# Attention of a transformer block on one core: pairs of heads in five pieces, projections in pieces of 24 products, one written order on TensorE, modulation vectors behind the projections

## The chip, the cores and the metric

The kernel runs on one core of a Trainium2 chip. A core has TensorE (PE in the profile), VectorE (DVE), ScalarE (ACT), GpSimd (POOL) and SyncE (SP), which here does nothing but issue loads. Each engine works through its own queue in order. The metric is the time of one execution on the device in microseconds (us); lower is better.

## The reference, cut to what matters

The program is a block of two layers over 256 latent and 256 context tokens with a model width of 1024. The first layer mixes by attention, the second by a gated recurrence (hgrn); each has a gated feed-forward part behind it (ffn). Modulation vectors, six for each layer, come from a condition vector:

```python
def ada_mod(cvec, w, b):
    return jnp.split(jax.nn.silu(cvec) @ w + b, 6, axis=-1)

q, k, v = jnp.split(h @ w_qkv, 3, axis=-1)         # 16 heads of 64
q = rms_norm(q.reshape(B, n, NA_HEADS, NA_HEAD_DIM), q_gain) * scale
k = rms_norm(k.reshape(B, n, NA_HEADS, NA_HEAD_DIM), k_gain)
...
s = jnp.einsum('bqhd,bkhd->bhqk', q_c, k_c)         # context tokens
p = jax.nn.softmax(s.astype(jnp.float32), axis=-1).astype(v_c.dtype)
o_c = jnp.einsum('bhqk,bkhd->bqhd', p, v_c)
out_ctx = o_c.reshape(B, h_ctx.shape[1], D_MODEL) @ w_o
...
s = jnp.concatenate([s_loc.reshape(B, NA_HEADS, GRID_W, n_loc), s_ctx], axis=-1)   # latent tokens
p = jax.nn.softmax(s.astype(jnp.float32), axis=-1).astype(v_win.dtype)
return (jnp.einsum('bhqjw,bjqwhd->bqhd', p_loc, v_win)
        + jnp.einsum('bhqk,bkhd->bqhd', p[..., n_loc:], v_c))
```

A latent token looks at a window of latent tokens, with a bias from a table, and at all context tokens; a context token looks at the context alone. Everything is in 32-bit floats.

## The kernel before

A 32-bit product is made of three matmuls on numbers split into a high and a low part (`prod`, high by high, high by low, low by high). "A product" below is one such matmul. The weights come by DMA as `w_raw` (1 MB for 1024 rows by 256 columns), are cast by ScalarE to `w_hi` and subtracted by DVE to `w_lo` (`weights`, `split`).

`na` is the attention. The 16 heads are handled as 8 pairs, in four groups g of two pairs. A group needs 256 columns each of q, k and v: for each of these, `toks` makes four token tiles of 24 products (8 tiles of the depth by 3), two token tiles to a bank of PSUM. The q and k banks are then normalized: ScalarE squares (`qk_sq`), DVE sums (`qk_ss`), takes an inverse root in nine small steps (`rsqrt`) and multiplies. v is copied by ScalarE. Group 0's columns are made earlier, in `setup`, and stand in banks (`early`).

`na_pair` does two heads. PE transposes q and k (8 transposes), ScalarE and DVE write the split `qs`, `ks`, `ql`. Then for each head a `chain`: scores of two query tiles against all 512 keys (`logits`, 8 matmuls of 512 columns for the pair), addition of the bias and minimum by DVE, exponential by ScalarE, scaling by DVE; 16 transposes of the probabilities (`turned`, copied to `pt_l` by ScalarE or DVE); scores of the context queries (8 matmuls of 256 columns), softmax, 8 transposes and a copy to `pt_c`; last the probabilities on the values (L651, L659) into a bank `o`, of which `oh` and `ol` are the high and low parts.

`ada` makes one modulation vector m of a layer. SP loads 8 tiles of 512 KB (`ada_raw`) into the pool `apool`, which has two buffers. For each tile PE makes four matmuls of 256 columns (L216; the trace lists 8 passes for a tile), side by side on four column groups. At the end DVE copies the row, PE transposes it (L228), and `ada_put` adds the bias. Before, `NA_ADA=((2,), (4,), (), (3,))` says which vector is made after which group: vector 2 with group 0, 4 with group 1, none with group 2, 3 with group 3.

Behind the groups stands the out-projection: its products (512 columns) multiply `w_o` and `oh`, `ol` of all eight pairs. Its product for pair k needs only that pair.

The order on the engines is not the order of the code. A scheduler of the framework takes the instructions by program order as a priority and by its own estimate of when operands are ready, and lets later products slip between the steps of attention. In the order that results before, products of the next group's projections and modulation steps stand singly and in small groups between the matmuls of attention, and the rest of a group's projections stand in a row ahead of the next group.

## Time and profile before

| | before |
|---|---|
| median of three runs | 1173.29 us |
| runs | 1167.57, 1173.29, 1173.75 us |
| profiled execution, time | 1168.13 us |
| profiled execution, span from first to last instruction | 1166.3 us |
| TensorE busy | 1138.9 us, 98% of the span |
| VectorE busy | 778.7 us, 67% |
| ScalarE busy | 501.7 us, 43% |
| 16 DMA engines | 145 GB/s on the mean |

"Busy" is the time in which an engine worked on at least one instruction. Matmuls overlap each other, so the mean length of one in the profile is more than the distance from one to the next; where density matters, the distance from start to start in the timeline is to be read. An execution takes some 2 us more than its span. All rows below are from the profiled execution, and times in them count from the start of its span.

### The profile page before, as it was taken

The page shows a single profiled execution, that of the slowest core. Times are in us where ns is not written, and L with a number is a line of the kernel's source. Part 1 is how long each engine was busy: PE and PEld are TensorE (multiplying, and loading weights), DVE is VectorE, ACT ScalarE, POOL GpSimd, SP SyncE. Part 2 cuts the span into 40 slices and gives each one's busy share as a digit, 9 for nine tenths or more (in the row PEclk, how much of TensorE's full clock was granted, in tenths as well). Part 3 has the DMA queues.
Part 4 walks back from the last instruction along what each step waited for, and adds up shares of the span by engine and source line. Part 5 has one row for each costly group of instructions (what it writes and reads, how often), then busy time and mean ns, then how long its engine had stood idle before and what let it go on. Part 6 is the DMA issues. An engine that isn't in the chain of part 4 may idle for free.

```text
span 1166.3 us, 21342 instructions
## 1 busy us (share of the span) xinstructions
PE 1138.9 (98%) x8539; PEld 987.2 (85%) x8539; DVE 778.7 (67%) x1872; ACT 501.7 (43%) x1079; POOL 74.5 (6%) x121
## 2 busy tenths in 40 slices
PE   6979989999999999999999999999999999999998
PEld 5968869887898787878887889889797988999998
DVE  4579776966697664845353778686768687556553
ACT  5356564745462232213223344434243465545442
POOL 1045331410000000000000000000000000000000
PEclk9999999999999999999999999999999999999999
DMA  9785452433337442636352651323232345564562
GB/s 330 252 211 94 118 131 73 64 130 124 107 93 229 135 170 94 230 136 216 130 194 68 199 167 46 100 74 110 73 110 74 99 175 197 182 210 158 197 217 87
DMA packets 134403, 169.23 MB, mean 145 GB/s; under 512 B 4609, under 2 KB 122273, under 8 KB 134305
## 3 DMA queue, kind: packets, MB, share of 16 engines
q1 hardware_dynamic: 132368, 164.64, 42.5%
q0 software_dynamic: 1728, 3.17, 3.2%
q8 instruction: 67, 1.10, 0.4%
q14 instruction: 32, 0.25, 0.1%
q10 hardware_dynamic: 208, 0.07, 0.0%
HBM read 166.82 MB, written 1.05 MB: 144 GB/s over the span
## 4 chain that ended last, share of the span: by engine, by line
PE 90%; DVE 4%; DMA 3%; ACT 2%; issue 1%; ACTq 0%; DVEq 0%
PE mm L410 49%; PE ax L410 28%; DMA ada_raw<-in_ada_w_dram 3%; PE ada_ps L216 2%; PE ax L651 2%; PE ax L902 1%; PE ax L613 1%; PE ax L579 1%; PE ax L637 1%; PE ax L885 1%; PE ax L580 1%; PE ada_ps L266 1%; ACT qs L569 1%; DVE w_lo L403 1%; PE ax L948 1%; PE ax L659 1%
## 5 line engine op out<-in xcount | busy, mean ns | idle before, releaser
L403 DVE TENSOR_TENSOR w_lo<-w_raw,w_hi 128x512 fp32r<-128x512 f32 (+1 forms) x448 | 272.5, 644 | 128.4 <-ACT w_hi L402 126.0
L402 ACT CAST w_hi<-w_raw 128x512 fp32r<-128x512 f32 (+1 forms) x448 | 238.0, 583 | 230.6 <-PE mm L410 100.3
L410 PE MATMUL mm<-hl,w_hi 128*128 128x256 f32 (+1 forms) x608 | 201.6, 333 | 0.0
L410 PE MATMUL mm<-hh,w_lo 128*128 128x256 f32 (+1 forms) x608 | 201.3, 332 | 0.0
L410 PE MATMUL mm<-hh,w_hi 128*128 128x256 f32 (+1 forms) x608 | 199.1, 329 | 0.0
L410 PE MATMUL ax<-hh,w_lo 128*128 128x256 f32 (+1 forms) x400 | 131.7, 330 | 0.0
L410 PE MATMUL ax<-hh,w_hi 128*128 128x256 f32 (+1 forms) x400 | 131.7, 329 | 0.0
L410 PE MATMUL ax<-hl,w_hi 128*128 128x256 f32 (+1 forms) x400 | 131.3, 328 | 0.0
L410 PE MATMUL mm<-w_hi,hh 128*128 128x256 f32 x448 | 126.3, 282 | 0.8 <-ACT hh L366 0.8
L410 PE MATMUL mm<-w_lo,hh 128*128 128x256 f32 x448 | 125.7, 280 | 0.0
L410 PE MATMUL mm<-w_hi,hl 128*128 128x256 f32 x448 | 125.5, 280 | 0.0
L410 PEld LDWEIGHTS mm<-hl,w_hi 128*128 128x128 f32 x608 | 114.1, 188 | 11.4
L410 PEld LDWEIGHTS mm<-hh,w_lo 128*128 128x128 f32 x608 | 114.0, 188 | 11.3
L410 PEld LDWEIGHTS mm<-hh,w_hi 128*128 128x128 f32 x608 | 113.8, 188 | 10.9 <-ACT hh L366 0.8
L319 DVE SCALAR_TENSOR_TENSOR ada_acc<-ada_raw,cs,ada_acc 128x1024 f32<-128x1024 f32 x63 | 79.0, 1280 | 19.4 <-DMA ada_raw<-in_ada_w_dram 19.2
L410 PEld LDWEIGHTS mm<-w_hi,hh 128*128 128x128 f32 x448 | 84.6, 189 | 5.1 <-issue 3.2
L410 PEld LDWEIGHTS mm<-w_hi,hl 128*128 128x128 f32 x448 | 84.2, 188 | 2.0 <-issue 1.6
L410 PEld LDWEIGHTS mm<-w_lo,hh 128*128 128x128 f32 x448 | 84.2, 188 | 1.8 <-issue 1.4
L410 PEld LDWEIGHTS ax<-hh,w_hi 128*128 128x128 f32 x400 | 75.2, 188 | 7.6 <-ACT w_hi L402 0.8
L410 PEld LDWEIGHTS ax<-hl,w_hi 128*128 128x128 f32 x400 | 75.1, 188 | 7.4
L410 PEld LDWEIGHTS ax<-hh,w_lo 128*128 128x128 f32 x400 | 74.9, 187 | 7.4 <-DVE w_lo L403 0.2
L696 ACT CAST mid_h<-sa 128x512 fp32r<-128x512 f32 (+1 forms) x44 | 22.5, 512 | 92.8 <-DVE sa L693 92.8
(278 smaller groups left out, 2133.3 us busy)
## 6 DMA issues: line engine op xcount, KB each, us to landing
w_raw<-in_ffn_w_in_dram SPq DMA_DIRECT2D x44, 1024.0 KB, 5.1
ada_raw<-in_ada_w_dram SPq DMA_DIRECT2D x80, 512.0 KB, 4.6
w_raw<-in_hg_w_in_dram SPq DMA_DIRECT2D x20, 1024.0 KB, 4.8
w_raw<-in_na_w_qkv_dram SPq DMA_DIRECT2D x9, 1024.0 KB, 5.0
ada_first<-in_ada_w_dram SPq DMA_DIRECT2D x32, 256.0 KB, 5.9
w_raw<-in_ffn_w_out_dram SPq DMA_DIRECT2D x8, 896.0 KB, 4.5
w_raw<-in_ffn_w_out_dram SPq DMA_DIRECT2D x8, 768.0 KB, 4.3
w_raw<-in_ffn_w_out_dram SPq DMA_DIRECT2D x8, 640.0 KB, 4.3
```

The source lines that it names most:

```text
L216: nc.tensor.matmul(ps[32 * j : 32 * j + 32, 0:256], cs[:, k, :], w[:, j * 256 : (j + 1) * 256], start=(k == 0), stop=(k == last), tile_pos ...
L266: nc.tensor.matmul(ps[32 * j : 32 * j + 32, 0:P], self.cs[:, k, :], w[:, j // 2, (j % 2) * P : (j % 2 + 1) * P], start=(k == 0), stop=(k = ...
L319: eng.scalar_tensor_tensor(acc[s], w, c, acc[s], op0=ALU.mult, op1=ALU.add)
L402: self.nc.scalar.copy(wh[:, ks], raw[:, ks])
L403: self.nc.vector.tensor_tensor(wl[:, ks], raw[:, ks], wh.bitcast(F32)[:, ks], op=ALU.subtract)
L410: self.nc.tensor.matmul(out, a, b, start=(start and i == 0 and j == 0), stop=(stop and i == n - 1 and j == 2), skip_group_check=True,)
L569: nc.scalar.activation(cap(qa[half], P - 1, back), src, AF.Copy, scale=self.q_gain[own])
L579: nc.tensor.matmul(ps, qs[a][:, t], ks[a][:, kr], start=True, stop=False, skip_group_check=True)
L580: nc.tensor.matmul(ps, self.ql[a][:, t], ks[a][:, kr], start=False, stop=True, skip_group_check=True)
L613: nc.tensor.transpose(tp[:, kt * P : (kt + 1) * P], sb[:, kt * P : (kt + 1) * P], self.ident)
L651: nc.tensor.matmul(o[64 * a : 64 * a + 64, 0:256], v[:, kt, j * P + 64 * a : j * P + 64 * a + 64], pts[a][0][:, kt], start=(kt == 0), stop ...
L696: nc.scalar.copy(mh, sa)
```

## The change

`na_pair` becomes a generator that gives way four times and so has five pieces: (1) the transposes of q and k with what ScalarE and DVE make of them; (2) the local scores and softmax of both heads; (3) the 16 transposes of the probabilities, the context scores and their softmax; (4) the context transposes; (5) the probabilities on the values. Within a piece both heads follow each other.

`pieces` cuts the projections of groups 1 to 3 into 36 pieces of 24 products, in the order v, q, k for each group, and gives `ada_steps(0, (2, 4, 3))` behind them. That makes the three modulation vectors of attention in twelve steps of two tiles (8 matmuls); its first turn only loads the first two tiles, and each step asks for the next two tiles behind its own matmuls. The pool has two buffers as before.

`na` then writes out which pieces of projections stand between which pieces of pairs: four before the first scores, and in a group 2, 2, 1, 1, 2, 1, 1 and 2 (`fill`). So groups 0 and 1 hold 12 pieces of projections each, group 2 has 8 and then the first modulation steps, and group 3 has the rest of these. The first piece of the next group's first pair stands in the second half of the group, between piece 3 and piece 4 of its second pair.

`in_order` adds to every PE instruction of this part an order dependency on the one before it. So PE's order is the written one there. The early projections and the out-projection are not in that list; the out-projection's products are still placed by the scheduler.

```diff
-NA_ADA = ((2,), (4,), (), (3,))
...
+    def ada_steps(self, l, params):
...
+        def pair(m, k):
+            ws = []
+            for e in range(2):
+                w = self.apool.tile([P, D], F32, name="ada_raw", tag="ada_raw")
+                nc.sync.dma_start(w, self.in_ada_w[l, (k + e) * P : (k + e + 1) * P, m * D : (m + 1) * D])
+                ws.append(w)
+            return ws
+
+        todo = [(m, k) for m in params for k in range(0, KT, 2)]
+        ws, turn = pair(*todo[0]), None
+        yield
+        for n, (m, k) in enumerate(todo):
+            if k == 0:
+                ps = self.psum.tile([P, T], F32, tag="ada", name="ada_ps", bufs=1)
+            for e, w in enumerate(ws):
+                for j in range(4):
+                    nc.tensor.matmul(
...
+            if n < len(todo) - 1:
+                ws = pair(*todo[n + 1])
+            if k == KT - 2:
+                row = self.spool.tile([P, 256], F32, name="ada_row", tag="ada_row", bufs=1)
+                nc.vector.tensor_copy(row, ps[:, 0:256])
+                yield
+                for b in range(2):
+                    nc.tensor.transpose(ps[:, 256 + b * P : 256 + (b + 1) * P], row[:, b * P : (b + 1) * P], self.ident)
+                self.ada_put(l, m, 0, 4, ps[:, 256:512], 0)
+            else:
+                yield
...
+    def in_order(self, first):
+
+        ins = [i for i in self.nc.cur_bb.bb.instructions[first:] if i.engine == mybir.EngineType.PE]
+        for i, j in zip(ins[:-1], ins[1:]):
+            self.tc.add_manual_dep(
+                j, i.name, mybir.DependencyInfo(mybir.DependencyClass.NoSync, mybir.DependencyReason.DATA),
+                reason="in_order",
+            )
...
+        blocks = [(g, i) for g in range(1, 4) for i in (2, 0, 1)]
...
+        def pieces():
+            load(0)
+            for n, (g, i) in enumerate(blocks):
+                for tt in range(4):
+                    if tt % 2 == 0:
+                        banks[g, i, tt // 2] = self.mm()
+                    self.toks(banks[g, i, tt // 2][:, tt % 2 * 256 : tt % 2 * 256 + 256], loaded[n], tt)
+                    if tt == 0:
+                        load(n + 1)
+                    yield
+            yield from self.ada_steps(0, (2, 4, 3))
...
+        for i in range(2):
+            for b in range(2):
+                normed(0, i, b)
+        for b in range(2):
+            values(0, b)
+        fill(2)
+        pair = [self.na_pair(np_, pr, done, oh, ol) for pr in range(2 * 4)]
+        next(pair[0])
+        values(1, 0)
+        fill(2)
+        values(1, 1)
         for g in range(4):
...
+            one, two = pair[2 * g : 2 * g + 2]
+            next(one)
+            fill(2)
+            next(one)
+            fill(2)
+            next(two)
+            next(one)
+            if g < 3:
                 for b in range(2):
...
+                    normed(g + 1, 0, b)
+            fill(1)
+            next(one, None)
+            fill(1)
+            if g < 3:
+                normed(g + 1, 1, 0)
+            next(two)
+            fill(2)
+            if g < 3:
+                normed(g + 1, 1, 1)
+            next(two)
+            fill(1)
+            if g < 3:
+                next(pair[2 * g + 2])
+            next(two)
+            fill(1)
+            next(two, None)
+            if g < 2:
+                values(g + 2, 0)
+            fill(2)
+            if g < 2:
+                values(g + 2, 1)
+        assert next(steps, steps) is steps
+        self.in_order(first)
```

What the change does to the order is seen best in three places. In these listings the line numbers are those of the kernel that is listed; L410, L554, L216, L637 and L651 of before are L445, L661, L322, L746 and L759 of the changed kernel, and `x4` means four in a row.

The first place is PE in the middle of attention, where the second pair of a group ends and the first pair of the next group begins (`ident,qk` are transposes of q and k, `ident,sbc` context transposes, `pt_l,v` probabilities on values). Before:

```order
L637 MATMUL ax_2702<-ident,sbc 128x128 x2
L651 MATMUL ax_2718<-pt_l,v 64x256 x4
L659 MATMUL ax_2718<-pt_c,v 64x256 x4
L554 MATMUL ax_2752<-ident,qk_2168 128x128 x4
L554 MATMUL ax_2753<-ident,qk_2315 128x128 x4
L410 MATMUL mm<-w_lo,hh_158 128x256
```

And the changed kernel:

```order
L445 MATMUL mm<-w_lo,hh_164 128x256
L445 MATMUL mm<-w_hi,hl_172 128x256
L661 MATMUL ax_2495<-ident,qk_2140 128x128 x4
L661 MATMUL ax_2496<-ident,qk_2253 128x128 x4
L746 MATMUL ax_2519<-ident,sbc 128x128 x4
L746 MATMUL ax_2525<-ident,sbc 128x128 x4
L445 MATMUL mm<-w_hi,hh_157 128x256
```

The transposes of the next group's q and k, which stood behind the last products on values of a group, now stand ahead of the context transposes, right behind a piece of products.

The second place is PE in the last group, whose modulation steps are `ada_raw,cs`; `oh` and `ol` are products of the out-projection. Before, near the transposes of the last pair:

```order
L554 MATMUL ax_3329<-ident,qk_2915 128x128 x4
L554 MATMUL ax_3330<-ident,qk_3062 128x128 x4
L216 MATMUL ada_ps<-ada_raw,cs 32x256 x8
L410 MATMUL mm<-oh_863,w_hi 128x512
L410 MATMUL mm<-ol_871,w_hi 128x512
```

And the changed kernel there, from the end of the seventh pair's context scores on:

```order
L688 MATMUL ax_3399<-ks_3215,ql_880 128x256
L322 MATMUL ada_ps<-ada_raw,cs 32x256 x16
L661 MATMUL ax_3458<-ident,qk_2887 128x128 x4
L661 MATMUL ax_3459<-ident,qk_2988 128x128 x4
L746 MATMUL ax_3482<-ident,sbc 128x128 x4
L746 MATMUL ax_3488<-ident,sbc 128x128 x4
L322 MATMUL ada_ps<-ada_raw,cs 32x256 x8
L759 MATMUL ax_3508<-pt_l,v 64x256 x8
L759 MATMUL ax_3508<-pt_c,v 64x256 x4
L333 MATMUL ada_ps<-ident,ada_row 128x128 x2
L322 MATMUL ada_ps<-ada_raw,cs 32x256 x8
```

Four steps (one step is x8) now stand in the stretch that had one.

The third place is the queue of SP from the start of attention on (`L298` and `L310` are loads of modulation tiles for attention). Before:

```order
L395 DMA w_raw<-in_na_w_qkv_dram 128x8x256 x2
L298 DMA ada_raw<-in_ada_w_dram 128x1024 x4
L395 DMA w_raw<-in_na_w_qkv_dram 128x8x256
L298 DMA ada_raw<-in_ada_w_dram 128x1024 x4
L395 DMA w_raw<-in_na_w_qkv_dram 128x8x256 x2
L395 DMA w_raw<-in_na_w_o_dram 128x8x256 x3
```

And the changed kernel:

```order
L430 DMA w_raw<-in_na_w_qkv_dram 128x8x256 x7
L430 DMA w_raw<-in_na_w_o_dram 128x8x256 x3
L310 DMA ada_raw<-in_ada_w_dram 128x1024 x2
L430 DMA w_raw<-in_na_w_o_dram 128x8x256
L310 DMA ada_raw<-in_ada_w_dram 128x1024 x20
```

The loads of modulation tiles, which stood among those of weights, now stand in a row behind them.

## Rows read from the trace of the kernel before

**Rows 1.** The page's busy times: us, share of the span, instructions.
```profile
PE 1138.9 (98%) x8539; PEld 987.2 (85%) x8539; DVE 778.7 (67%) x1872; ACT 501.7 (43%) x1079; POOL 74.5 (6%) x121
```

**Rows 2.** The page's chain that ended last, by engine and line.
```profile
PE mm L410 49%; PE ax L410 28%; DMA ada_raw<-in_ada_w_dram 3%; PE ada_ps L216 2%; PE ax L651 2%; PE ax L902 1%; PE ax L613 1%; PE ax L579 1%; PE ax L637 1%; PE ax L885 1%; PE ax L580 1%; PE ada_ps L266 1%; ACT qs L569 1%; DVE w_lo L403 1%; PE ax L948 1%; PE ax L659 1%
```

**Rows 3.** Stretches of attention: length, busy us (instructions) of each engine, clock, DMA.
```profile
195.50:250.90 55.40, 54.95 (x434) 48.71 (x433) 43.93 (x130) 33.48 (x72) 16.57 (x20) 1.00 0.35 72
250.90:291.00 40.10, 40.04 (x271) 27.68 (x269) 27.42 (x71) 25.67 (x58) 0.00 (x0) 1.00 0.40 132
sum 229.00, PE 218.98 PEld 177.78 DVE 174.81 ACT 128.36 POOL 67.82; mean PE 43.80 PEld 35.56 DVE 34.96 ACT 25.67 POOL 13.56
```

**Rows 4.** Waits from 62 to 291 us: total us, times, longest.
```profile
PE ada_ps L216 <- DMA ada_raw<-in_ada_w_dram: 9.1, 6, 2.6
```

**Rows 5.** Waits of SP's own queue in the same stretch.
```profile
SPq L298 <- PE ada_ps L216: 39.0, 14, 10.7
SPq L298 <- DMA ada_raw<-in_ada_w_dram: 28.9, 10, 8.4
```

**Rows 6.** PE's timeline (start, us, operation): first transposes of groups 2 and 3.
```profile
195.47 1.03 PE L554 MATMUL ax<-ident,qk 128*128 128x128 f32 x8
...
249.22 0.28 PE L410 MATMUL mm<-w_hi,hh 128*128 128x256 f32 x1
...
250.93 1.03 PE L554 MATMUL ax<-ident,qk 128*128 128x128 f32 x8
```

**Rows 7.** Group 2's operations on PE by form: count, busy us, mean ns.
```profile
L410 PE MATMUL mm<-w_lo,hh 128*128 128x256 f32 x97 | 27.1, 280 | 0.0
```

**Rows 8.** PE's timeline around a modulation step of the last group.
```profile
264.78 0.28 PE L579 MATMUL ax<-ks,qs 128*128 128x256 f32 x1
264.90 0.28 PE L580 MATMUL ax<-ks,ql 128*128 128x256 f32 x1
...
265.35 1.07 PE L216 MATMUL ada_ps<-ada_raw,cs 128*32 128x256 f32 x16
...
266.69 0.39 PE L410 MATMUL mm<-oh,w_hi 128*128 128x512 f32 x1
266.92 0.40 PE L410 MATMUL mm<-ol,w_hi 128*128 128x512 f32 x1
```

**Rows 9.** PE's timeline at the start of attention: first modulation step, first scores.
```profile
62.75 1.07 PE L216 MATMUL ada_ps<-ada_raw,cs 128*32 128x256 f32 x16
...
81.58 0.40 PE L579 MATMUL ax<-ks,qs 128*128 128x512 f32 x1
```

**Rows 10.** DVE's timeline at the start of attention, with idle time before in brackets.
```profile
74.87 0.69 DVE L481 TENSOR_REDUCE qk_ss<-qk_sq 128x8 f32<-128x512 f32 x1 [2.24 <-ACT qk_sq L479]
...
76.84 0.69 DVE L484 TENSOR_TENSOR qk<-ax,rq_y 128x512 f32<-128x512 f32 x1
```

**Rows 11.** Group 2's operations on DVE by form.
```profile
L484 DVE TENSOR_TENSOR qk<-mm,rq_y 128x512 f32<-128x512 f32 x4 | 2.8, 692 | 1.8 <-PE ax L554 1.6
...
L619 DVE COPY pt_l<-ax 128x512 f32<-128x512 f32 x4 | 2.7, 677 | 0.1
L633 DVE TENSOR_REDUCE sm_mc<-ax 128x2 f32<-128x512 f32 x4 | 2.7, 673 | 0.0
L586 DVE TENSOR_SCALAR sbc<-sbc,sm_l 128x256 f32<-128x256 f32 x8 | 2.6, 347 | 0.0
```

**Rows 12.** PE's timeline at the end of attention.
```profile
288.22 1.73 PE L651 MATMUL ax<-pt_l,v 128*64 128x256 f32 x13
...
290.96 0.50 PE L410 MATMUL mm<-ol,w_hi 128*128 128x512 f32 x1
```

**Rows 13.** SP's timeline in the last group, and its modulation loads from issue to landing.
```profile
266.05 0.80 SPq L298 DMA_DIRECT2D ada_raw<-in_ada_w_dram  x2
...
DMA to landing us min/median/max: 3.7/4.8/5.0
```

**Rows 14.** A stretch of group 1 with two waits of PE for modulation tiles.
```profile
151.00:158.50 7.50, 4.34 (x42) 2.38 (x39) 3.44 (x9) 4.82 (x8) 4.08 (x4) 1.00 0.58 197
```

189 lines of the change are left out of this document (91 added, 98 removed).

## The prediction, made before the changed kernel had run

> **What bounds the kernel now.** I read the page first: its busy shares and the granted clock, then the chain that ended last, then a table of stretches through attention, the waits of TensorE and SyncE there, and single rows of the timelines. TensorE (PE) is busy 98% of the span [rows 1], at a granted clock of 1.00, the full 2.4 GHz, in the stretches read [rows 3, 14], and the chain that ended last is mostly PE's own products; the only foreign entry of weight is the load of modulation tiles, `ada_raw`, with 3% [rows 2]. So only what makes PE idle, or makes it do the same products less densely, can move the time. Attention lies between 62 and 291 us, and of its 229.0 us PE is idle 229.0 - 219.0 = 10 [rows 3]. Nearly all of that is one wait, PE's for modulation tiles, 9.1 us in 6 waits [rows 4]. It has a cause that the change touches: two buffers hold these tiles, so SyncE (SP) can issue the next load only when the matmuls on an older tile are over; SP waited 39.0 us for them and 28.9 us for earlier landings [rows 5]. The other thing to see is how dense attention is. Group 2, which has no modulation vectors, lasts from 195.47 to 250.93, 55.5 us [rows 6]; its 97 + 97 + 96 products (one of three such rows stands in [rows 7]) follow each other at 0.114 us in a row (15 of them from 249.22 to 250.93, [rows 6]); I take 0.1155 with their switches. They take 33.5, so a pair of heads costs (55.5 - 33.5) / 2 = 11.0.
>
> **The change part by part.** No product, matmul, copy or load is added or removed: 36 pieces of 24 products are the 864 of before, and 12 steps of 8 matmuls are the 96 on modulation tiles. What changes is when PE does what, and that its order inside attention is now fixed, so that a late operand stops all that stands behind it.
>
> *Pieces instead of a mixture, a gain.* A pair has 40 narrow passes of PE (8 and 16 transposes, 8 context scores, 8 context transposes) at 0.12 us from start to start [rows 8], 4.8 us; 8 scores of 512 columns at 0.23 (the step of two 512-wide rows there), 1.85; 24 passes of probabilities on values, 2.75 (the last pair's fill 288.22 to 290.96, two of them apart from the rest, [rows 12]); with some 0.3 for switches, 9.7. That is 1.3 less than the 11.0 of before, times 8 pairs 10 us. A group of 288 products and two pairs would take 33.3 + 19.4 = 52.7, dense.
>
> *The start: a small gain.* The early products end at 62.75, where before a modulation step of two tiles stands [rows 9]. Now 48 products stand there, to 68.2. Then PE comes to the transposes of the first pair, which need the normalized q and k. VectorE (DVE) is the late one: before, it ended the last of these at 76.84 + 0.69, because the sums of group 1's squares went first, one of them at 74.87 after a wait of 2.24 [rows 10]. Now nothing of group 1's q or k is queued there, and I work the chain out at 74.2. PE stands idle some 6 us for it, where before it stood idle for tiles. 0.5 of transposes and 48 products of 5.5 bring the first scores to 80.3, before 81.58 [rows 9]. Bounds: 77.5 instead of 74.2 (+3.3), or 72 (-2).
>
> *Groups 0 and 1: the wait for k.* In the second half of a group the pieces of the next group's k end 33.8 us after its first scores, and PE comes to the next pair's transposes at 40.0. In between DVE has k's own chain (square on ScalarE 0.6, sum 0.68, some nine small steps of 0.2, product 0.69: 3.8), but also, queued with it, two `pt_l` copies of 0.68, two context minima of 0.67, and softmax scalings and sums of about 1.9 [rows 11]: 4.6 together. k is ready at 33.8 + 8.4 = 42.2, and PE waits 2.2. Behind the waiting transposes all of PE's order is queued, products too. Period 52.7 + 2.2 = 54.9. Bounds 52.7 (DVE takes k's chain first) and 57.3 (twice the wait). First scores of group 2: 80.3 + 2 x 54.9 = 190.1. In group 2 this wait is covered: the order puts 23 products of the out-projection into the middle of these transposes. From the scores of group 2 to the first modulation step there are 8 pieces (22.2), 23 products of 0.231 (5.3) and two pairs less one product on values (16.4, 0.2 of switches left out): 43.9, so the step starts at 234.0.
>
> *The last group: a new chain of loads, and the largest term.* From 234.0 PE has left: 12 steps at 1.0 ([rows 8]: 16 passes in 1.07, its end overlapped), 2.75 of the pair before, 8.7 and 9.7 for the last two pairs, 40 products (9.2) and three pairs of row transposes: 43.3 in all. If no tile were ever late, attention would end at 277.5, against 290.96 [rows 12]: 13.5 us gained. But before, the 24 modulation tiles were spread over 62 to 274; now 20 loads in a row stand at the end of SP's queue, and each of them waits for the matmuls that free its buffer. From the start of a step to the issue of the reload pass 0.70 us (265.35 on PE to 266.05 on SP), and from issue to landing 3.7 to 5.0, median 4.8 [rows 8, 13]. So a buffer comes round in 4.4 (0.70 + 3.7) to 5.5 us (0.70 + 4.8). I take 4.6, near the low end, since the later of two transfers issued together makes the median and here the first tile of a step decides. The work that the order places between the first matmuls of two steps is 1.0 to 4.1 us in ten of eleven intervals (16 transposes and 8 context scores with the step: 4.0; nothing but the step, between steps 5 and 6: 1.0), so a dense PE waits in these; only the one with 24 out-projection products is longer, 6.6. Eleven rounds of 4.6 are 50.6; 2.0 are added for the long interval and 2.7 (an estimate) for the two places where a finished vector is copied by DVE, transposed and added before its bank can take the next one. The last step starts at 234.0 + 55.3; its two tiles take 1.7, and behind it stand the row copy, the last context transposes, ScalarE's copy and the last products on values, 5.2. End of attention 234.0 + 62.2 = 296.2. At 4.4 it is 294, at 5.5 it is 306.
>
> *After attention.* The first product that needs the last pair waits for its two halves, 0.85 (an estimate: a copy and part of another of the size of `pt_l` in [rows 11]); 63 of the out-projection's products are done by then, 59 before, 4 x 0.231 = 0.92 back. Together nothing. The modulation vectors are needed from the out-projection's end on, some 40 us later, so their lateness costs nothing. ScalarE and DVE have the same work.
>
> **Sum:** 296.2 - 290.96 + 0.85 - 0.92 = +5.2 us. Against the profiled execution's 1168.13 that is 1173.3; that execution lies 5.2 under the median of the three runs, 1173.29, and on that the forecast is 1178.
>
> *A page on the load.* The row says 3.7 to 5.0 us for 512 KB on the hardware queue [rows 13]. The Trainium skill, "DMA: Bandwidth & Descriptors", section "Anatomy of one DMA — SWDGE (gpsimd) path", gives about 2.0 us plus bytes over 436 GB/s, for the other kind of queue; from that I estimate 3.2, a round of 3.9, and a change of about -2 us in place of +5, inside rival 2's reach. The rows lie above it, and the sum goes by them.
>
> **Rivals.**
> 1. *The loads are hidden, faster.* Place: the eleven rounds. Price: all waiting in the tail, 62.2 - 43.3 = 18.9, so an end at 277.5, -13.5 (1155 on the profiled execution, 1160 on the median). It decides from a round of about 3.3 us, the mean work per step. For it: the rows of the landing come from stretches with up to four tiles and a 1 MB load on the queue, and now only two tiles are in flight. Against it: the shortest landing there is 3.7, and short intervals (1.0 between steps 5 and 6) would still wait. With a round of 3.9 to 4.2 the result is between: -2 to +1.
> 2. *Level.* DVE's chain for k does not delay PE (period 52.7, -4.4), or the round is 4.2: 1173 to 1175. For it: DVE is busy 44 of 55 us in group 2 [rows 3], so it has slack.
> 3. *More waiting.* Both tiles of a step are loaded one behind the other at the median, round 5.5, +15; or k's wait doubles, +10. 1183 to 1189.
> 4. *The clock falls, slower.* If bursts of 1 to 4 us between waits made the clock drop to 1.2 GHz from 234 us on, intervals with 4 us of work would take 8: six of them and the end give +20 to +30, 1195 to 1208. Against it: from 151 to 158.5 PE was busy 4.34 of 7.5 us around two such waits, at a granted clock of 1.00 [rows 14]. The Trainium skill, "TensorE: Matmul & The Clock Gate", section "HAM oscillation — how this bites in real kernels", tells of just this form, short bursts of matmuls between waits for loads that leave each burst at the half clock. By that rule this rival would be the likeliest; the trace so far does not agree, though with one stretch only.
>
> **How the numbers follow.** About 0.5% (6 us) is what a measurement of this kernel can tell from no change. The forecast (+2 to +9) has 0.42, rival 1 has 0.17, rival 2 0.17, rival 3 0.17, rival 4 0.07. The forecast's centre, +5, lies just under the bound, so its chance is split in two. Faster by over 0.5%: rival 1 and a little of rival 2, 0.18. Within: half of the forecast and most of rival 2, 0.40. Slower: the rest, 0.42. The range leaves out the far end of rival 1 and rival 4, and reaches over rival 3: 1162 to 1192.
>
> **What would show it right or wrong.** In the profile of after, PE should be nearly without waits between 80 and 230 us save 2 us before the transposes of groups 1 and 2; the first scores at 80, those of group 2 near 190; the first modulation step near 234. From there PE's waits for `ada_raw` should be near 15 to 19 us in about ten waits, SP's loads should come every 4.6 us, each 0.7 behind a step, and the last products on values should end near 296. Wrong would be: tiles that land in under 3.3 us; a clock under 1.00 after 234; or a group much longer than 55, with PE waiting for q or k.

## The result and the profile after

| | before | after |
|---|---|---|
| median | 1173.30 us | 1191.57 us |
| ratio, 95% interval | | 1.0162 (1.0127 to 1.0196) |
| span of the profiled execution | 1166.3 us | 1185.7 us |
| TensorE busy in it | 1138.9 us | 1136.9 us |

The changed kernel is 1.6% slower. The forecast was 1178, with a range of 1162 to 1192. The page of after (busy times, clock in 40 slices, the chain's shares):

```profile
PE 1136.9 (96%) x8539; PEld 994.4 (84%) x8539; DVE 776.9 (66%) x1872; ACT 499.9 (42%) x1079; POOL 75.0 (6%) x121
...
PEclk9989999998899999999999999999999999999999
...
PE 85%; DVE 8%; DMA 4%; ACT 2%; issue 1%; ACTq 0%; DVEq 0%; SPq 0%
```

TensorE is busy for about the same time [rows 1], and its idle time grew by 21 us, from 27.4 to 48.8; DVE's share of the chain went from 4% to 8%. New against before is the clock: three slices show 8 tenths. Three waits of TensorE from 60 to 315 us (total, times, longest) answer to the one of [rows 4]:

```profile
PE ada_ps L322 <- DMA ada_raw<-in_ada_w_dram: 14.1, 10, 3.5
PE ax L661 <- DVE qk L550: 9.7, 4, 4.6
PE ax L661 <- DVE rq_b L475: 4.4, 1, 4.4
```

The waits for modulation tiles did not go; they grew from 9.1 to 14.1 us. The waits of the transposes of q and k for DVE, at the start (4.4 and 0.5) and ahead of groups 1 to 3 (2.4, 4.6, 2.1), are new. The stretches of attention (length, then busy us of PE, PEld, DVE, ACT, POOL, clock, DMA share, GB/s) show how the time divides:

```profile
75.00:137.00 62.00, 58.70 (x472) 54.99 (x472) 46.75 (x133) 36.36 (x77) 26.51 (x30) 0.96 0.38 68
137.00:196.00 59.00, 54.37 (x441) 50.91 (x440) 45.02 (x130) 32.86 (x72) 17.18 (x20) 0.97 0.35 68
196.00:242.70 46.70, 44.57 (x337) 40.84 (x335) 42.44 (x127) 30.49 (x68) 16.72 (x20) 0.98 0.37 63
242.70:313.40 70.70, 54.12 (x400) 32.70 (x399) 25.59 (x73) 21.53 (x51) 0.00 (x0) 0.87 0.61 194
```

The last one runs from the first modulation step to the end of attention. In [rows 3] no stretch has a clock under 1.00, and the last group there is busy 40.04 of 40.10 us. Against the forecast's marks:

| | forecast | after |
|---|---|---|
| first scores | 80.3 | 80.9 |
| group 0, first scores to first scores | 54.9 | 56.9 |
| group 1 | 54.9 | 58.2 |
| group 2, first scores to first modulation step | 43.9 | 46.7 |
| from there to the end of attention | 62.2 | 70.6 |
| end of attention to end of span, against before's 875.3 | 875.2 | 872.4 |

The end of attention is taken here as the start of the first product behind the last products on values, so the 70.6 hold a wait of 0.7 that the forecast counted behind attention. Two places were sized too small, the waits for k with what follows them, by 8 us, and the last group, by 8.

### The profile page after: what moved, and what is told of

Its sections match the earlier page's. It is cut to its first block, busy times and chain, and to the rows that moved or that the text cites. A ratio compares the mean times of both kernels' runs of the same rounds, so it can differ in the third digit from the quotient of the medians.

```text
span 1185.7 us, 21326 instructions
## 1 busy us (share of the span) xinstructions
PE 1136.9 (96%) x8539; PEld 994.4 (84%) x8539; DVE 776.9 (66%) x1872; ACT 499.9 (42%) x1079; POOL 75.0 (6%) x121
## 4 chain that ended last, share of the span: by engine, by line
PE 85%; DVE 8%; DMA 4%; ACT 2%; issue 1%; ACTq 0%; DVEq 0%; SPq 0%
PE mm L445 48%; PE ax L445 26%; DMA ada_raw<-in_ada_w_dram 3%; DVE w_lo L438 2%; PE ax L759 1%; PE ax L722 1%; PE ax L1002 1%; PE ada_ps L322 1%; PE ax L687 1%; PE ax L688 1%; DMA w_raw<-in_hg_w_in_dram 1%; PE ax L985 1%; PE ada_ps L265 1%; PE ax L746 1%; PE ax L1048 1%
## 5 line engine op out<-in xcount | busy, mean ns | idle before, releaser
L445 PE MATMUL mm<-hl,w_hi 128*128 128x256 f32 (+1 forms) x608 | 201.5, 333 | 0.0
L445 PE MATMUL mm<-hh,w_lo 128*128 128x256 f32 (+1 forms) x608 | 200.8, 331 | 0.0
L445 PE MATMUL mm<-hh,w_hi 128*128 128x256 f32 (+1 forms) x608 | 198.7, 328 | 0.0
L445 PE MATMUL ax<-hh,w_lo 128*128 128x256 f32 (+1 forms) x400 | 131.2, 328 | 0.2 <-DVE w_lo L438 0.2
L445 PE MATMUL ax<-hh,w_hi 128*128 128x256 f32 (+1 forms) x400 | 131.1, 328 | 0.0
L445 PE MATMUL ax<-hl,w_hi 128*128 128x256 f32 (+1 forms) x400 | 131.0, 328 | 0.0
L445 PE MATMUL mm<-w_hi,hh 128*128 128x256 f32 x448 | 128.7, 287 | 0.8 <-ACT hh L401 0.8
L445 PE MATMUL mm<-w_lo,hh 128*128 128x256 f32 x448 | 126.9, 283 | 0.0
L445 PE MATMUL mm<-w_hi,hl 128*128 128x256 f32 x448 | 126.8, 283 | 0.0
L445 PEld LDWEIGHTS mm<-hl,w_hi 128*128 128x128 f32 x608 | 114.2, 188 | 11.2
L445 PEld LDWEIGHTS mm<-hh,w_lo 128*128 128x128 f32 x608 | 114.3, 188 | 10.9
L445 PEld LDWEIGHTS mm<-hh,w_hi 128*128 128x128 f32 x608 | 113.8, 188 | 11.2 <-ACT hh L401 0.8
L354 DVE SCALAR_TENSOR_TENSOR ada_acc<-ada_raw,cs,ada_acc 128x1024 f32<-128x1024 f32 x63 | 79.0, 1280 | 19.4 <-DMA ada_raw<-in_ada_w_dram 19.2
L445 PEld LDWEIGHTS mm<-w_hi,hh 128*128 128x128 f32 x448 | 86.5, 193 | 4.0 <-issue 2.7
L445 PEld LDWEIGHTS mm<-w_lo,hh 128*128 128x128 f32 x448 | 86.2, 192 | 0.4 <-issue 0.2
L445 PEld LDWEIGHTS mm<-w_hi,hl 128*128 128x128 f32 x448 | 85.8, 192 | 0.4 <-issue 0.4
L445 PEld LDWEIGHTS ax<-hh,w_hi 128*128 128x128 f32 x400 | 75.2, 188 | 7.9 <-ACT w_hi L437 0.8
L445 PEld LDWEIGHTS ax<-hh,w_lo 128*128 128x128 f32 x400 | 75.1, 188 | 7.4 <-DVE w_lo L438 0.4
L445 PEld LDWEIGHTS ax<-hl,w_hi 128*128 128x128 f32 x400 | 75.2, 188 | 7.3
```

What stands on the lines that cost most here:

```text
L354: eng.scalar_tensor_tensor(acc[s], w, c, acc[s], op0=ALU.mult, op1=ALU.add)
L445: self.nc.tensor.matmul(out, a, b, start=(start and i == 0 and j == 0), stop=(stop and i == n - 1 and j == 2), skip_group_check=True,)
```

## The experiments

Ratios are to the kernel before, run on the same chip in the same batch; the changed kernel stands at 1.0162.

### The reloads in the last group

`reuse`: the two tiles of the first step are used in all twelve steps.

```diff
             if n < len(todo) - 1:
-                ws = pair(*todo[n + 1])
+                pass
```

> The changed kernel with the 24 modulation tiles of attention replaced by two that are loaded once (22 loads of 512 KB left out, so the modulation vectors are made of the wrong rows; same matmuls, same order). Theory (two buffers: each step waits for its reload, 14.1 us, and the clock falls behind the longest of these waits, some 7 us): the last group shrinks from 70.6 us to about 49, 1168 to 1173 in all, no granted clock under 1.00 after 245 us. Rival (in the last group the pieces wait for softmax on VectorE and ScalarE anyway, the tiles only come last): at most 10 us faster, 1181 or more.

Measured: 0.9952 (0.9935 to 0.9970), 1165.55 us, faster than even the theory had it. The last group took 39.6 us, where the changed kernel took 69.6. (Here and below the last group is counted from its first modulation step to the start of its last product on values; the 69.7 of the expectations is this stretch.) TensorE's largest waits in `reuse`:

```profile
PE ax L661 <- DVE qk L550: 10.5, 4, 4.6
PE ax L661 <- DVE rq_b L475: 4.4, 1, 4.4
```

and its last group, as a stretch:

```profile
245.30:286.00 40.70, 40.21 (x383) 26.13 (x383) 25.21 (x73) 21.23 (x51) 0.00 (x0) 0.98 0.15 53
```

No wait for softmax took the reloads' place, as the rival had it: TensorE is busy 40.2 of 40.7 us. Not all of the 30 us are the reloads' own. While tiles are late in the changed kernel, the scheduler lets 63 products of the out-projection start before the last product on values, and in `reuse` 43; the other 20, 4.6 us at 0.23 each [rows 8], stand behind attention there. The reloads themselves are worth some 25 us, which is also what the two ratios differ by. Some 16 of these are idle time in the changed kernel (54.12 busy of 70.70); in the other 9 TensorE is busy, but with slow work behind the waits (clock 0.87). Whether this slow work takes time of its own is tried under the clock, below.

How they come to cost that was tried with one tile a step. `onefirst` and `onefirst2` meant to give the first tiles one buffer:

```diff
-                nc.sync.dma_start(w, self.in_ada_w[l, (k + e) * P : (k + e + 1) * P, m * D : (m + 1) * D])
-                ws.append(w)
+                if e == 0:
+                    nc.sync.dma_start(w, self.in_ada_w[l, (k + e) * P : (k + e + 1) * P, m * D : (m + 1) * D])
+                    ws.append([w[:, 0:512], w[:, 512:1024]])
+                else:
+                    ws.append(self.x[0:2])
...
```

> The changed kernel in which the second tile of each modulation step is never loaded; its matmuls read two tiles of the residual stream that lie in memory anyway (12 loads left out, so the modulation vectors are wrong; same matmuls, same order, one buffer for the first tiles as before). The modulation steps of the changed kernel came every 5.8 us in the last group, not every 4.6. Theory (the first tile comes after 4.5, as forecast; the second one comes 1 to 2 us later and stands, with the work that TensorE's order has behind it, in series to the next round): waits for tiles fall from 14 us to 7, first step to last product on values from 69.7 us to 57 to 62, 1177 to 1184. Rival (the first tiles alone set the rate): 67 us or more, 1188 or more.

```diff
+                    nc.gpsimd.memset(w[:, 0:1], 0.0)
                     ws.append(self.x[0:2])
```

> The changed kernel with only the first tile of each step loaded, as in the earlier run of that kind, but with the other buffer held by a tile of which one column is set (there the first tiles had both buffers in turn, so each was loaded a step ahead). The second half of a step reads the residual stream (12 loads left out, wrong modulation vectors). Theory (the first tile alone gives rounds of 4.5 where nothing else is late; the second tile's landing and the work behind it came in series on top): first step to last product on values 55 to 62 us in place of 69.7, 1177 to 1184, and the difference to the earlier run, 12 us or more, is what one step of lookahead is worth. Rival (a step's second tile hides behind the first one's reload): 66 us or more, 1188 or more.

Measured: 0.9980 (0.9960 to 1.0001) and 0.9943 (0.9927 to 0.9959), last group 43.3 and 42.2 us. Both fell below what theory and rival had, and the loads show why: two were in flight (in `onefirst` one was issued at 248.57, the next at 249.43, and they landed at 254.74 and 255.99), so the pool, it seems, gave its free buffer to the next first tile. So neither is the test that was meant; what they show is that with half the loads and one step of lookahead the waits for tiles nearly vanish (2.4 and 2.2 us). `onefirst3` loads into one tile by name:

```diff
+        one = self.apool.tile([P, D], F32, name="ada_raw", tag="ada_raw")
...
+            nc.sync.dma_start(one, self.in_ada_w[l, k * P : (k + 1) * P, m * D : (m + 1) * D])
+            return [[one[:, 0:512], one[:, 512:1024]], self.x[0:2]]
...
```

> The changed kernel with only the first tile of each step loaded, all into one and the same buffer, so that each load waits for the step before, as the first tiles do in the changed kernel (in the two earlier runs of this kind the loads came two deep); the second half of a step reads the residual stream (12 loads left out, wrong modulation vectors). Theory (rounds of 4.5 where the reload sets them, the longer of reload and work elsewhere; the second tile and the work behind it came in series on top in the changed kernel): first step to last product on values 54 to 62 us, against 69.7 with two tiles and 43 with a step of lookahead; 1177 to 1184. Rival (the second tile hides behind the first one's reload): 66 us or more, 1188 or more.

Measured: 1.0038 (1.0021 to 1.0056), 1178.41 us, last group 57.1 us. Its waits and its loads:

```profile
PE ada_ps L320 <- DMA ada_raw<-in_ada_w_dram: 7.2, 6, 3.2
```

```profile
DMA to landing us min/median/max: 3.4/3.6/4.0
```

First tiles came every 4.6 us (eleven rounds in 50.6), as in the forecast. In the changed kernel the rounds are 5.75. But `onefirst3` takes away two things at once, the wait for a second tile and the second load in flight. With two in flight, in the changed kernel, a tile took longer to land:

```profile
DMA to landing us min/median/max: 3.6/4.4/5.5
```

The changed kernel's timeline on TensorE tells more:

```profile
261.94 0.64 PE L322 MATMUL ada_ps<-ada_raw,cs 128*32 128x256 f32 x8 [1.45 <-DMA ada_raw<-in_ada_w_dram]
...
264.82 1.08 PE L322 MATMUL ada_ps<-ada_raw,cs 128*32 128x256 f32 x8 [1.26 <-DMA ada_raw<-in_ada_w_dram]
267.09 1.08 PE L322 MATMUL ada_ps<-ada_raw,cs 128*32 128x256 f32 x8 [1.19 <-DMA ada_raw<-in_ada_w_dram]
268.10 3.48 PE L722 MATMUL ax<-ident,sb 128*128 128x128 f32 x16
...
272.46 1.07 PE L322 MATMUL ada_ps<-ada_raw,cs 128*32 128x256 f32 x16
276.99 0.64 PE L322 MATMUL ada_ps<-ada_raw,cs 128*32 128x256 f32 x8 [3.46 <-DMA ada_raw<-in_ada_w_dram]
278.22 1.08 PE L322 MATMUL ada_ps<-ada_raw,cs 128*32 128x256 f32 x8 [0.59 <-DMA ada_raw<-in_ada_w_dram]
...
283.85 0.64 PE L322 MATMUL ada_ps<-ada_raw,cs 128*32 128x256 f32 x8 [1.00 <-DMA ada_raw<-in_ada_w_dram]
...
289.36 0.64 PE L322 MATMUL ada_ps<-ada_raw,cs 128*32 128x256 f32 x8 [0.86 <-DMA ada_raw<-in_ada_w_dram]
...
294.84 0.64 PE L322 MATMUL ada_ps<-ada_raw,cs 128*32 128x256 f32 x8
297.59 0.64 PE L322 MATMUL ada_ps<-ada_raw,cs 128*32 128x256 f32 x8 [2.11 <-DMA ada_raw<-in_ada_w_dram]
300.15 1.08 PE L322 MATMUL ada_ps<-ada_raw,cs 128*32 128x256 f32 x8 [1.92 <-DMA ada_raw<-in_ada_w_dram]
```

The rows at 297.59 and 300.15 are the two tiles of one step. Their loads, each with the time from issue to landing:

```profile
293.84 0.33 SPq L310 DMA_DIRECT2D ada_raw<-in_ada_w_dram  x1
DMA to landing us min/median/max: 3.7/3.7/3.7
295.54 0.33 SPq L310 DMA_DIRECT2D ada_raw<-in_ada_w_dram  x1
DMA to landing us min/median/max: 4.6/4.6/4.6
```

The first tile came round in 4.45 us (293.14 to 297.59), near the forecast's 4.6. The second one took longer: its matmuls began at 294.84, its reload was issued 0.70 later, landed after another 4.6, and the next second tile began at 300.15, a round of 5.31. In seven of the eleven rounds the second tile began right at its landing, 5.1 to 5.6 us after the second tile of the step before. There the later tile of a step sets the round, and the work does hide behind its reload. In the other four rounds, 5.8 to 7.1 us long, work stood before the second tile when it had landed. One of them starts at 267.09: the second tile had come 2.3 us after the first, and only behind it could the 16 transposes, at half clock, and the 8 scores run, so that lag and work add up. The next tile waited for no load at 272.46.

### The wait for k

`klate` and `kmid` move the transposes of the next group's q and k back, `klate` behind the context transposes and one piece, `kmid` behind one more piece, with the context transposes behind it too. The edit of `klate`, then that of `kmid`:

```diff
             fill(1)
+            next(two)
+            fill(1)
             if g < 3:
                 next(pair[2 * g + 2])
-            next(two)
-            fill(1)
             next(two, None)
```

```diff
             next(two)
-            fill(1)
+            fill(2)
             if g < 3:
                 next(pair[2 * g + 2])
             next(two)
-            fill(1)
             next(two, None)
```

> The changed kernel with the first piece of the next group's first pair (transposes of q and k) moved behind the context transposes of the pair before and one piece of 24 products. Theory (TensorE waits at these transposes for VectorE's product on k, 2.4, 4.6 and 2.1 us, and the clock falls behind each of the three): these waits go below 1 us, the clock stays at 1.00 between 80 and 245 us, and the kernel is 9 to 14 us faster, 1178 to 1183. Rival (the wait moves to the scores, whose qs and ks are now written later): 3 us or less, 1188 or more.

> The changed kernel with the transposes of the next group's q and k and the context transposes of the pair before both behind one more piece of 24 products (the piece that stood between context transposes and products on values goes there). Theory (both VectorE chains, the product on k and the scaling of the context probabilities, get 2.8 us more): waits for k at groups 1 and 2 fall from 2.4 and 4.6 to under 2.5 together, no wait for the context probabilities as in the run with the later transposes (6.6 us there), and the time is 5 to 9 us under the changed kernel, 1180 to 1184. Rival (VectorE is behind by its total work, and every delay is followed by the next one): 2 us or less.

Measured: `klate` 1.0120 (1.0093 to 1.0146), `kmid` 1.0113 (1.0071 to 1.0154), by the ratios 5 and 6 us less than the changed kernel, whose interval (1.0127 to 1.0196) overlaps with both, so that neither gain is clear of the noise. For `klate` the time lies between theory and rival, for `kmid` it is the theory's, though not by its waits. In `klate` the wait for k is 0.6 us, as expected, but the context transposes, which now stood earlier, waited for DVE:

```profile
PE ax L746 <- DVE sbc L694: 4.3, 6, 1.6
PE ax L746 <- DVE sm_l L693: 2.3, 4, 0.7
```

In `kmid` k was still awaited for 5.0 us in three waits, where under 2.5 were expected. The trace of after says why DVE is that late. DVE's rows, then those of GpSimd and TensorE in the same stretch:

```profile
176.23 0.79 DVE L474 TENSOR_TENSOR rq_b<-rq_y 128x8 f32<-128x8 f32 x1
...
177.48 0.98 DVE L694 TENSOR_SCALAR sbc<-sbc,sm_l 128x256 f32<-128x256 f32 x1
178.38 0.15 DVE L474 TENSOR_TENSOR rq_b<-rq_y 128x8 f32<-128x8 f32 x1
...
179.36 1.15 DVE L438 TENSOR_TENSOR w_lo<-w_raw,w_hi 128x512 fp32r<-128x512 f32 x1
```

```profile
175.91 2.40 POOL L645 TENSOR_SCALAR tb<-tb 128x768 f32<-128x768 f32 x1 [4.85 <-DMA tb<-in_na_rpb_dram]
178.38 1.59 POOL L648 TENSOR_SCALAR_AFFINE_SELECT tb<-tb 64x576 f32<-64x576 f32 x2
```

```profile
182.04 0.44 PE L661 MATMUL ax<-ident,qk 128*128 128x128 f32 x2 [4.63 <-DVE qk L550]
```

The same small operation takes 0.79 us at 176.23 and 0.15 at 178.38; the scaling takes 0.98 for 0.35 [rows 11]. GpSimd is at work on the next pair's bias table just then. `notb` leaves that work out:

```diff
-        nc.gpsimd.tensor_scalar_mul(tb[:, 0:768], tb[:, 0:768], -1.0)
-        for u in range(2):
-            q = slice(64 * u, 64 * u + 64)
-            nc.gpsimd.affine_select(
...
```

> The changed kernel without GpSimd's work on the bias table (one scaling and four masks a pair left out, so the scores' bias and window are wrong; its loads stay). In the trace of the changed kernel DVE's operations are longer while GpSimd works on the table: from 176.2 to 181 us five of them take 0.63, 0.63, 0.49, 0.48 and 0.53 us more than the same form does elsewhere, 2.8 us, in the very chain that makes k for group 2, where TensorE waits 4.6 us; at group 1 only one is longer and the wait is 2.4. Theory (the half of the k wait that the forecast lacked is this collision): the wait at group 2 falls to 1.5 to 2.5 us, that at group 1 by 0.5, and the kernel is 3 to 5 us faster, 1186 to 1189. Rival (DVE's operations are long for another reason, such as late inputs): waits as before, within 1.5 us.

Measured: 1.0078 (1.0050 to 1.0107), 1179.44 us, some 10 us less than the changed kernel, where 3 to 5 were expected. DVE's own busy time fell by as much, from 776.9 to 766.9 us, and in the changed kernel DVE waited nowhere between 75 and 245 us for the table; so its longer operations cost the time, and not a late table. The scaling's group on DVE from 176 to 182 us in the changed kernel, and from 170 to 177 in `notb`, at the same place of the program:

```profile
L694 DVE TENSOR_SCALAR sbc<-sbc,sm_l 128x256 f32<-128x256 f32 x4 | 2.5, 626 | 0.0
```

```profile
L681 DVE TENSOR_SCALAR sbc<-sbc,sm_l 128x256 f32<-128x256 f32 x4 | 1.4, 346 | 0.0
```

Its waits for k are 3.7 us in two, 1.9 each, and groups 0 and 1 take 54.0 us each; the forecast had 2.2 and 54.9. So work of DVE and GpSimd at the same time is what the forecast lacked there.

### The clock

Behind the waits the granted clock falls. Three stretches of after (at 124 and 240, behind the waits of 2.44 and 2.13 us for k of groups 1 and 3, and at 264 in the last group):

```profile
124.00:128.00 4.00, 4.00 (x22) 4.00 (x23) 3.25 (x5) 3.35 (x6) 3.10 (x3) 0.57 0.43 129
240.00:244.00 4.00, 3.57 (x26) 2.55 (x26) 3.43 (x6) 3.60 (x6) 0.00 (x0) 0.57 0.00 0
264.00:270.00 6.00, 3.99 (x25) 2.34 (x26) 0.17 (x1) 0.59 (x1) 0.00 (x0) 0.53 0.66 185
```

`keep` fills the waits with idle matmuls, whose results nothing uses (`spare(n)` makes n of them); `keep2` has fewer of them, and `notb_keep` is `keep2` without the table work. The edit of `keep` is shown without the idle matmuls ahead of modulation tiles, of which there are eight groups (not nine, as the expectation says).

```diff
+        spare(36)
         next(pair[0])
...
             if g < 3:
+                if g < 2:
+                    spare((20, 38)[g])
                 next(pair[2 * g + 2])
```

> The changed kernel with idle matmuls put into TensorE's order just ahead of the matmuls that waited in the trace after: 36 ahead of the first pair's transposes (the wait there was 4.4 us), 20 and 38 ahead of the transposes of groups 1 and 2 (waits 2.4 and 4.6), 4 to 28 ahead of nine modulation tiles. Each is 256 columns, 0.115 us, on operands that are long there, and each group is shorter than the wait it stands in, so no work of the kernel should come later. Theory A (the clock): behind each wait the granted clock was 0.5 for some 4 us, and work there took twice as long; I count 15 us of that from start-to-start times. With the clock kept up this kernel should be 10 to 14 us faster than the changed kernel, 1178 to 1182. Theory B (the waits alone: the slow stretches only eat into the next wait): no change, 1190 to 1193.

> The changed kernel with fewer idle matmuls than in the first run of that kind, each group clearly shorter than its wait, only where slow work follows on the path: 30 ahead of the first pair's transposes, 30 ahead of group 2's, 6 to 16 ahead of five tiles in the last group. Theory C (in the first such run some of them were longer than the wait and gave back what the clock gained; two stretches of the last group run 1.9 and 2.3 us slow, others hide behind the next reload): 3 to 6 us less than the changed kernel. Theory B (slow stretches only eat into the next wait): within 2 us of it.

> The same with the idle matmuls of the second run of that kind (30, 30, and 6 to 16 ahead of five tiles). In that run the start, group 1 and the last group were 1.4, 1.5 and 1.4 us shorter than in the changed kernel, and group 0, which held none, 4.3 longer, with DVE's chain for k under GpSimd's work. Theory D (the clock is worth about 4 us in all, and the collision took them back): 3 to 5 us less than the kernel that only leaves out the table work. Rival (the clock costs nothing on balance): within 1.5 us of it.

Measured: `keep` 1.0162 (1.0139 to 1.0184) with a mean clock of 0.996 for 0.986; `keep2` 1.0195 (1.0169 to 1.0221) at 0.994; `notb_keep` 1.0085 (1.0058 to 1.0111) at 0.997, `notb` 1.0078 at 0.990. The clock came back and the time did not. So theory A fell, and the gains that `keep2` (theory C) and `notb_keep` (theory D) were expected to bring did not come either. In the last group the effect is within 1.5 us: 69.9 and 68.2 us with idle matmuls, 69.6 without, and 67.8 against 68.0 in the last two runs. Theory B holds there: slow work mostly eats into the next reload. In `keep`, with the clock up, at least eight of the eleven second tiles still began within 0.1 us of their landing, in rounds of 4.9 to 5.6. A small part is left: behind the slow matmuls at 267.09 the reload was issued 1.14 us after their start, and not 0.70.

Elsewhere the slow work does not count as nothing: in `notb_keep` the first scores came 1.3 us earlier after the end of the setup than in `notb`, and group 1 took 1.5 longer, since 30 idle matmuls (3.5 us) were longer than its wait of 1.9. For the falls behind the waits for k no run separates the clock from the wait itself. By arithmetic, 4 us at 0.57 are 1.7 lost at each of groups 1 to 3, 5 of the 11 us that `notb` gained up to the first modulation step; the shorter waits (9.2 to 3.7) are the other 5.5. That division was only argued.

### The order and the place

`b_last` is the kernel before with the modulation vectors behind the last group; `noorder` is the changed kernel without its fixed order.

```diff
-NA_ADA = ((2,), (4,), (), (3,))
+NA_ADA = ((), (), (), (2, 4, 3))
```

```diff
-        self.in_order(first)
```

> The kernel before with only its table changed: all three modulation vectors behind the last group, order left to the scheduler. Theory (the placement of the loads costs only where the order is fixed ahead of attention; here out-projection products can stand between): 1163 to 1176, TensorE's waits for tiles 10 us or less, clock 1.00. Rival (the placement alone is the loss, 22 reloads in a row on two buffers): 1183 or more, with waits for tiles above 14 us after 250 us.

> The changed kernel without the dependencies that fix TensorE's order; pieces, their place in the program and the two buffers stay. Theory (the loss is a fixed order that puts late modulation tiles ahead of work that is ready): the scheduler moves modulation steps behind out-projection products as it did in the kernel before, and the time is that of before within 0.5%, 1165 to 1176, with at most 6 us of waits for tiles. Rival (the pieces and the place of the modulation vectors are the loss, whatever orders them): 1183 or more.

Measured: `b_last` 1.0007 (0.9995 to 1.0019), `noorder` 0.9973 (0.9949 to 0.9997), both as the theories had it. The modulation matmuls of `noorder` (first and last start):

```profile
L322 PE MATMUL ada_ps<-ada_raw,cs x192: 379/379/403, 228.9 to 296.3; 128*32 128x256 f32 x192
```

They go on after the last products on values (from 279.9 us), among out-projection products, and the waits for tiles are 5.0 us. In `b_last` they run from 87.3 to 308.4, past the last products on values (from 282.3), with 3.4 us of waits. So neither the place of the vectors nor the pieces lose the time; a fixed order that puts late tiles ahead of ready work does.

### What a fixed order can give

`best1` is `kmid` with eight modulation steps behind every fourth piece of groups 0 to 2 and four in the last group. `best2` has three pieces ahead of the first pair. `best3` also gives the transposes of a finished row and its addition a turn of their own. `reuse_kmid` joins `reuse` and `kmid`. The edits of `best1`, `best2` and `best3`:

```diff
+        ada = self.ada_steps(0, (2, 4, 3))
...
+                    if 4 * n + tt in (0, 4, 8, 12, 16, 20, 24, 28, 32):
+                        next(ada)
                     yield
-            yield from self.ada_steps(0, (2, 4, 3))
+            for turn in range(16):
+                if turn in (1, 5, 9, 13):
+                    next(ada, None)
+                yield
+            yield from ada
...
```

```diff
-        fill(2)
+        fill(3)
         pair = [self.na_pair(np_, pr, done, oh, ol) for pr in range(2 * 4)]
```

```diff
                 self.ada_put(l, m, 0, 4, ps[:, 256:512], 0)
+                if n < len(todo) - 1:
+                    yield
...
-                    if 4 * n + tt in (0, 4, 8, 12, 16, 20, 24, 28, 32):
+                    if 4 * n + tt in (0, 4, 8, 12, 16, 18, 20, 24, 28, 32, 34):
...
-                if turn in (1, 5, 9, 13):
+                if turn in (1, 5, 9, 13, 15):
```

> The order of the run before (one more piece ahead of the transposes), and the modulation steps no longer in a row at the end: eight of the twelve stand one behind every fourth piece of projections in groups 0 to 2, the last four in every fourth turn of the last group. Two buffers, all loads, fixed order. Theory (a reload of some 4.6 us is hidden when 11 us of other work stand between two steps): waits for tiles under 3 us, the last group from its first scores to its last product on values takes 30 to 36 us in place of 55, and the time is 1157 to 1167. Rival (the last group needs the steps as filling while softmax runs): the last group stays above 40 us with waits for VectorE and ScalarE, 1168 to 1176.

> The same with three pieces in place of two ahead of the first pair's transposes, every later piece one turn earlier. Theory (TensorE waits 4.4 us there for VectorE, a piece takes 2.8): 2 to 4 us less than the run without it. Rival (the bank for the third piece, or its weights, come as late as q and k): no change within 1 us.

> The run with three pieces at the start and spread modulation steps, with one more edit: the transposes of a finished modulation row and the addition behind them get a turn of their own, two to three pieces before the next vector's first matmul, where they stood right ahead of it. Theory (TensorE waited 3.1 us there for VectorE to release the bank): 2 to 5 us less than that run, no wait for that addition. Rival (VectorE's order keeps the addition late anyway): within 1.5 us.

> Both suspected costs taken away: two modulation tiles loaded once and used for all steps (22 loads left out, wrong modulation vectors), and the transposes of the next group behind one more piece. Theory (the two costs are apart: some 25 us for the reloads and 9 us for k): 1155 to 1160. Rival (one wait hides the other): 1163 or more.

Measured: 0.9932 (0.9915 to 0.9949); 0.9888 (0.9855 to 0.9922); 0.9885 (0.9862 to 0.9907), 1156.26 us; 0.9910 (0.9875 to 0.9945), 1157.78 us. In `best1` no wait for tiles is left, and the last group takes 30.5 us from its first scores; `best2` took 4 us more off the median. `best3` removed the wait for the addition but is level with `best2` in the ratio, so that edit's gain is not shown. `reuse_kmid` came out as the theory had it: its two costs are apart. The page of `best3` and its two largest waits of TensorE in attention:

```profile
PE 1127.8 (98%) x8539; PEld 988.9 (86%) x8539; DVE 784.9 (68%) x1872; ACT 498.8 (43%) x1079; POOL 74.7 (6%) x121
```

```profile
PE ax L768 <- ACT pt_c L758: 3.2, 3, 1.4
PE ax L696 <- DVE ol L775: 2.0, 3, 1.0
```

Here the gain that the forecast named shows: 1127.8 us busy against 1138.9 before [rows 1], with the same work. It takes the pieces and the written order together; `noorder`, with the same pieces, is busy 1136.8. `best2` and `best3` are 1.1% faster than the kernel before.

## Why the prediction was right or wrong

The direction of the forecast's centre held, its size did not: +5 us forecast, +18 measured, at the end of the range. The waits for tiles came nearly as forecast, 14.1 us in ten for 15 to 19 in about ten, and that says little: in the last group TensorE was busy 54.1 us with what the forecast counted as 43.3, and this slow work fills time in which it would otherwise wait.

- *Pieces instead of a mixture*: right. `notb`'s groups of 54.0 us, a wait of 1.9 in each, against 55.5 before, and `best3`'s busy time, show it.
- *The start*: the number was right, 80.9 for 80.3, partly by luck. The setup, which the change does not touch, ended at 61.69 in this execution and at 62.75 before [rows 9]; from there the first scores took 19.2 us, where the forecast had 17.6. The wait for DVE was there (4.4 + 0.5 us). The fall of the clock behind it was not in the sum; with idle matmuls in that wait (`notb_keep`) it is 17.5.
- *Groups 0 and 1, the wait for k*: this step failed. The chain on DVE was costed with durations from means [rows 11]; with GpSimd's table work beside it single operations took up to five times as long (0.79 us for 0.15), the waits were 2.4 and 4.6 for 2.2 each, and 2.1 came ahead of group 3, where the forecast thought the wait covered. With the clock's falls behind them that is 8 of the 14 us by which the span was missed. The bound of 57.3 held for group 0 and not for group 1.
- *The last group*: that the reloads set the rounds was right, their size was not. The step that failed is "here the first tile of a step decides", on which the round of 4.6 rests. The first tile alone does give 4.6 (`onefirst3`, 57.1 us for the group). With two tiles the second one decides: with two loads in flight it lands in 4.4 to 4.7 us in the rounds that it sets, and comes round in 5.1 to 5.6 us in seven of eleven rounds; in the other four the work between the tiles is longer still. From the first step to the last the forecast had 55.3 us (eleven rounds of 4.6 and 4.7 for special places), and 63.3 were measured: 8 us more. This is the bound of 5.5 and the first half of rival 3, to which, with its other half, 0.17 was given.
- *After attention*: forecast as nothing, and 2.9 us less were measured. That is chance in this one execution: by the same mark seven variants of the changed kernel that leave that part as it is (`onefirst3`, `klate`, `kmid`, `keep`, `keep2`, `notb`, `notb_keep`) take 874.3 to 875.1 us, near the 875.2 of the forecast.
- *Rival 1, hidden loads*: fell; `reuse` prices them at 25 us of the whole. *Rival 2, level*: fell. *Rival 4, the clock*: its mechanism appeared, its price did not. Not the whole tail but some 4 us behind each longer wait ran at half clock, and in the last group holding the clock up gave back 1.5 us at the most. The Trainium skill, "TensorE: Matmul & The Clock Gate", section "HAM oscillation — how this bites in real kernels", tells of bursts between waits for loads that each start at the half clock, at a cost in time. The trace agrees on the fall (0.53 from 264 to 270 us), and the runs do not on the cost here.
- *On the load*: from the fit that the Trainium skill, "DMA: Bandwidth & Descriptors", section "Anatomy of one DMA — SWDGE (gpsimd) path", gives for the other kind of queue, the estimate was 3.2 us; 3.4 to 4.0 were measured with one tile in flight, so the rows were the better base.
- Two of its sums are slightly off, 80.3 (the terms give 80.2) and 277.5 (277.3); nothing hangs on them.

## What to carry to other kernels

An order written by hand on one engine is only as good as its latest operand: put into it only what is surely there, and keep a step of lookahead for every load that stands in it. When a step has several operands with reloads of their own, cost its round by the one that lands last, with the landing time of that many loads in flight, and add the work that can start only behind it. And cost a chain on VectorE with the rows of the stretch where GpSimd works, not with means.

## What the runs showed of the hardware

GpSimd's work on its table in memory held VectorE's operations up: 0.79 us for 0.15, 0.98 for 0.35, and 626 ns against 346 on the mean when that work was left out; 10 us of the whole kernel hung on it. The Trainium skill, "SBUF — State Buffer", section "SBUF: two separate sides", says that the two engines share a pair of ports that one holds for a whole instruction. The trace agrees that they hold each other up. It does not show that this lasts a whole instruction: five VectorE operations between 176.94 and 177.48 us kept their usual lengths (0.14 to 0.34 us) while GpSimd's operation of 2.40 us was on.

Two tiles of 512 KB in flight landed later than one: 3.6 to 5.5 us, median 4.4, in the changed kernel, and 3.4 to 4.0, median 3.6, in `onefirst3`.

TensorE's granted clock averaged 0.57 over the 4 us behind waits of 2.1 to 4.6 us in the changed kernel, mostly the lower of its two levels, 1.2 GHz, while in the kernel before the two waits in [rows 14] left it at 1.00. The longer of these two:

```profile
156.46 0.64 PE L216 MATMUL ada_ps<-ada_raw,cs 128*32 128x256 f32 x8 [2.57 <-DMA ada_raw<-in_ada_w_dram]
```

It is longer than the wait of 2.13 us behind which the clock fell. The length of a single wait does not tell by itself.
